# Two-layer decoder trunk on one core: five of sixteen expert pairs returned to the tokens by way of DRAM, and the later adaLN vectors computed on VectorE, ScalarE and GpSimd

## The chip, the core and the metric

One core of a Trainium2 chip runs the whole program. The metric is the device time of one execution in microseconds (us); the time before is the median of three. The engines are TensorE (PE, matrix products; its weight loads are listed as PEld), VectorE (DVE), ScalarE (ACT), GpSimd (POOL) and SyncE (SP), and sixteen DMA engines move data between DRAM and the on-chip memory. Each engine works through its own instructions in order and waits at semaphores for the others.

## What is computed

Two layers work on 512 tokens of width 1024 in float32. A conditioning vector gives six vectors (shift, scale and gate for the mixer, and for the experts) in each layer. A mixer of stick-breaking attention and gated linear attention follows, then 32 experts, of which each token uses two.

```python
def reference(x, c, w_ada, b_ada, norm_mix, norm_ffn, w_in, ...):
    c_act = jax.nn.silu(c)
    for l in range(DEPTH):
        mod = (c_act @ w_ada[l] + b_ada[l])[:, None, :]
        shift_m, scale_m, gate_m, shift_f, scale_f, gate_f = jnp.split(mod, N_MOD, axis=-1)
        h = rms_norm(x, norm_mix[l]) * (1.0 + scale_m) + shift_m
        x = x + gate_m * hybrid_mixer(h, w_in[l], ...)
        h = rms_norm(x, norm_ffn[l]) * (1.0 + scale_f) + shift_f
        x = x + gate_f * hierarchical_moe(h, ...)
    return x

# hierarchical_moe: comb is nonzero for two of the 32 experts of a token
    for g in range(N_GROUPS):
        a = jnp.einsum('nd,edf->nef', hf, w_gate[g])
        u = jnp.einsum('nd,edf->nef', hf, w_up[g])
        y = y + jnp.einsum('nef,efd->nd', jax.nn.silu(a) * u * comb[:, g, :, None], w_down[g])
```

## The kernel before

Each layer has a mixer stage and an expert stage.

**The mixer.** `project` cuts the input projection into steps of 128 rows of `w_in`. Two rows of steps share one load into a tile of the ring `raw` (4 tiles of 512 KB); ScalarE and VectorE split each part into a high and a low half, `whl` (lines 95 and 96), and TensorE multiplies (line 74). `mixer` walks through the steps: it loads 6 steps ahead, splits 2 steps ahead, runs the step, and advances the attention's generators. From step 12 on it also advances the generator `later`, which holds the conditioning vectors that are not needed at once: 12 chunks of 512 columns in layer 0 (eight of its own, four of layer 1) and 8 in layer 1. `paid` sets the pace, 1.1 pulls a step in layer 0 and 0.95 in layer 1.

A chunk is one call of `ada` (lines 220 to 256). It loads 2 MB of `w_ada` as four tiles `wada` of two row sets each. The first four chunks of layer 0 and six of layer 1 take them from the ring `mixs` (6 tiles), the others from `raw`, the ring of the projection's weights. TensorE then multiplies them by the conditioning vector in eight products, two passes each, that fill 32 rows of a PSUM bank each; ScalarE copies the bank to `row` (line 245), and a product with `sel` (ones in four rows) sums it and turns it into columns or into a broadcast row. A chunk takes five pulls.

**The experts.** Tokens are sorted into 64 slots for each expert; experts are handled in 16 pairs, so that a pair fills 128 rows. `fetch` gathers a pair's tokens by an indirect DMA of GpSimd from the DRAM copy `xg`. For a pair, `hidden` (`gu`, line 78) multiplies with both input matrices, `turn` transposes (`hsT`), and `down` (`d`) multiplies with the output matrix, weighted by the router into `o` (line 1057). `combine` brings a pair's result back to the tokens by TensorE: `o` is split into `ohi` (ScalarE, line 1062) and `olo` (GpSimd, line 1063), eight units of two products with the 0/1 matrix `oT` (`y`) follow, and VectorE adds each unit to `x` (line 1070). Within a layer the order is gu(0), d(0), gu(1), y(0), d(1), gu(2), y(1), and so on.

Weights stream on SP's queue in one fixed order, two input matrices `wgu` and then two output matrices `wd` for each pair, into 5 tiles of 2 MB and 4 tiles of 1 MB. A load is issued when the tile it takes has been read for the last time: `wgu` after the `gu` of its pair, `wd` after its `d`. A load that waits holds up all that stand behind it.

A scheduler sets the order of most instructions; those given to `pm` and `kept_dma`, the expert products among them, keep the order of the program.

Of the kernel before, what the change touches and what calls it, by code (L numbers as in the profile page):

```python
# [9 lines left out]
F = mybir.dt.float32  # L10
# [15 lines left out]
NX = 16  # L26


@with_exitstack
def hybrid_decoder_kernel(ctx, tc, x, c, w_ada, b_ada, norm_mix, norm_ffn, w_in, w_gk2, b_gk, q_gain,  # L30
# [182 lines left out]
    xg = dram.tile([S, D], F, name="xg")  # L213

# [8 lines left out]
    def ada(l, c0, n, raw, bank, at, later=True):  # L223

        vec, half = c0 // D, c0 % D // 512
        src = w_ada[l].rearrange("(p k) n -> p k n", k=KT)
        product = pm if later else mm
        ws, m = {}, 1024 // n
        for k in range(0, KT, m):
            w = raw([P, m, n], name="wada")  # L230
            (SY.dma_start if later else lambda *a: kept_dma(SY, *a))(w, src[:, k:k + m, c0:c0 + n])
            for i in range(m):
                ws[k + i] = w[:, i]
            if later and k % 4 == 2:
                yield
        if later and vec in (2, 5) and not half:
            gates[l, vec] = (gts if vec == 5 else gms[l])([P, D])
            kept_dma(G, gates[l, vec], along(b_ada, l * 6 * D + vec * D, D))
        yield
        row = rowt[at]([P, n], name="row")  # L240

        ps = bank("ada")
        for k in range(KT):
            product(ps[32 * (k % 4):32 * (k % 4) + 32, 0:n], ct1[:, k:k + 1].to_broadcast([P, 32]), ws[k], k < 4, k >= 4)
        A.copy(row, ps[:, 0:n])
        yield
        if vec in (2, 5):
            ps = bank("adaG")
            product(ps, sel, row, True, True)
            g = gates[l, vec][:, 512 * half:512 * half + 512]  # L250
            V.tensor_tensor(g, ps, g, op=OP.add)
        else:
            ps = bank("adaT")
            for i in range(n // P):
                product(ps[:, i:i + 1], row[:, P * i:P * i + P], sel[:, 0:1], i == 0, True)
            modulation(l, vec, slice(c0 % D // P, (c0 % D + n) // P), ps)
        yield
# [25 lines left out]
    def mixer(l, xt, ss, x_src, pool, later):  # L283
# [504 lines left out]
        for i, (weight, _, _, run) in enumerate(steps):  # L788
# [13 lines left out]
            if i >= 12:  # L802
                paid += 0.95 if l else 1.1
                while paid >= 1:
                    paid -= 1
                    next(later, None)
# [53 lines left out]
    def moe(l, xt, ss, pool):  # L860
# [176 lines left out]
        def down(hT, ws, i=None):  # L1037
# [7 lines left out]
            for q in range(2):  # L1045
# [5 lines left out]
                o = ot([P, 512], name="o")  # L1051
# [43 lines left out]
        def combine_last(pairs):  # L1095
# [18 lines left out]
            for n, u in ((0, 5), (0, 6), (1, 0), (1, 1), (0, 7), (1, 2), (1, 3), (1, 4), (1, 5), (1, 6), (1, 7)):  # L1114
                unit(n, u)

# [82 lines left out]
        with tc.issue_after(listed.ins), tc.issue_after(normed.ins):  # L1199
# [16 lines left out]
            dump(f"cw{l}", cw)  # L1216
            exw = tmp.rearrange("p t k e -> p (t k) e")
# [22 lines left out]
        hs = None  # L1240
        for i in range(NE // 2):
# [8 lines left out]
            if i:  # L1250
                part = places(i - 1), down(hT, [loaded.pop((1, e)) for e in (2 * i - 2, 2 * i - 1)], i - 1)
            *_, hs = hidden(gT1 if i == 1 else now, 0 if i < 2 else P * (i % 2), [loaded.pop((0, e)) for e in (2 * i, 2 * i + 1)])
# [3 lines left out]
            if i == NE // 2 - 1:  # L1256
                break

            if i == 0:
                for _ in second:  # L1260
                    pass
                weights_by_slot()
            for u in range(4):
                for v in range(2):
                    if i:
                        combine(2 * u + v, *part)
                next(rest, None)
                if u == 2:
                    hT = turn(hs)
        last = []  # L1270
# [95 lines left out]
```

## Time and profile before

| what | us |
|---|---|
| median of three runs | 1231.82 (1229.91 to 1234.94) |
| the profiled execution | 1231.71, of which span 1229.6 |
| PE busy | 1176.4 (96%) |
| DVE busy | 687.8 (56%) |
| ACT busy | 472.6 (38%) |
| POOL busy | 188.2 (15%) |

The span is the time from the first to the last instruction of the profiled execution. Busy time counts the stretches in which an engine works on at least one instruction; matrix products overlap, so a group's mean duration is longer than the time between two of them. The profile cuts the span into 40 slices: TensorE is at nine tenths or more in nearly all, and the DMA engines are at that in the two expert stages (some 390 to 600 us and 980 to 1200 us) and moderate in the mixers.

### The profile page before, as it was taken

The numbers are of one execution on the slowest core, as the hardware profiler recorded it, in microseconds if no ns is written. First come the engines' busy times: TensorE is split into PE (matmuls) and PEld (weight loads), VectorE is DVE, ScalarE is ACT, GpSimd is POOL, SyncE is SP. The second block draws the span as 40 slices with busy tenths as digits, with TensorE's granted clock in tenths as the row PEclk, the third lists the DMA queues.
The fourth block names the chain that finished last, engine by engine and source line by source line (L and its number), as shares of the span: only waits on it lengthen the run. The fifth ranks groups of instructions, "written<-read, shape, count | busy, mean of one in ns | idle before, by whom it ended". The sixth has DMA issues, their size and how long they took to land. (4 is left out here: it accounts for less than half of the span.)

```text
span 1229.6 us, 17212 instructions
## 1 busy us (share of the span) xinstructions
PE 1176.4 (96%) x6441; PEld 743.4 (60%) x6441; DVE 687.8 (56%) x1343; ACT 472.6 (38%) x940; POOL 188.2 (15%) x222
## 2 busy tenths in 40 slices
PE   4999999999989999999999997999999999999996
PEld 2687766666765444444478785666776744444443
DVE  4475545465864555555566563445846565555553
ACT  4376646453242111111155764454624411111111
POOL 1000010011302222221110001001310222222110
PEclk8999999999999999999999999999999999999999
DMA  9653665643687999999445354564129599999981
GB/s 299 211 181 110 202 166 155 198 152 96 258 353 265 410 411 420 420 419 418 178 168 167 96 172 108 171 179 127 56 103 383 212 397 420 420 418 420 420 328 69
DMA packets 105902, 312.27 MB, mean 254 GB/s; under 512 B 12852, under 2 KB 49912, under 8 KB 81240
## 3 DMA queue, kind: packets, MB, share of 16 engines
q1 hardware_dynamic: 96920, 289.62, 63.3%
q0 software_dynamic: 8896, 21.52, 5.2%
q8 instruction: 52, 0.85, 0.3%
q14 instruction: 34, 0.28, 0.1%
HBM read 311.08 MB, written 8.40 MB: 260 GB/s over the span
## 5 line engine op out<-in xcount | busy, mean ns | idle before, releaser
L78 PE MATMUL gu<-wgu,gT 128*64 128x512 f32 x1024 | 225.4, 592 | 0.1
L74 PE MATMUL proj<-whl,hh 128*128 128x512 f32 (+2 forms) x768 | 220.6, 370 | 0.1
L78 PEld LDWEIGHTS gu<-wgu,gT 128*64 128x64 f32 x1024 | 75.4, 137 | 143.7 <-issue 142.2
L74 PEld LDWEIGHTS proj<-whl,hh 128*128 128x128 f32 x768 | 133.9, 190 | 35.0 <-issue 13.3
L1070 DVE TENSOR_TENSOR x<-y,x 128x512 f32<-128x512 f32 x240 | 148.2, 679 | 0.9 <-PE y L78 0.9
L74 PE MATMUL proj<-whl,hl 128*128 128x512 f32 (+2 forms) x384 | 138.6, 362 | 0.0
L1025 DVE TENSOR_TENSOR hs<-hs,gu 128x256 f32<-128x256 f32 x32 | 13.5, 421 | 201.2 <-ACT hs L1024 201.2
L78 PE MATMUL d<-wd,hT 128*64 128x512 f32 x512 | 116.9, 598 | 1.4 <-ACT hT L1034 1.4
L1063 POOL TENSOR_TENSOR olo<-o,ohi 128x512 fp32r<-128x512 f32 x60 | 77.0, 1285 | 263.4 <-ACT ohi L1062 263.4
L96 DVE TENSOR_TENSOR whl<-raw,whl 128x512 fp32r<-128x512 f32 (+2 forms) x128 | 73.2, 574 | 78.0 <-ACT whl L95 67.6
L78 PE MATMUL y<-ohi,oT 128*128 128x512 f32 x240 | 104.5, 436 | 0.0
L95 ACT ACTIVATE whl<-raw 128x512 fp32r<-128x512 f32 (+2 forms) x128 | 66.4, 524 | 76.6 <-PE proj L74 64.7
L78 PE MATMUL y<-olo,oT 128*128 128x512 f32 x240 | 94.2, 393 | 0.0
L74 PEld LDWEIGHTS proj<-whl,hl 128*128 128x128 f32 x384 | 72.4, 189 | 14.2 <-issue 4.3
L1024 ACT ACTIVATE hs<-gu 128x256 f32<-128x256 f32 x32 | 12.3, 385 | 168.4 <-PE gu L78 168.4
L78 PEld LDWEIGHTS d<-wd,hT 128*64 128x64 f32 x512 | 33.9, 136 | 62.2 <-issue 48.1
L78 PEld LDWEIGHTS y<-ohi,oT 128*128 128x128 f32 x240 | 45.4, 189 | 31.7 <-issue 26.0
L1003 ACT ACTIVATE gT<-g,mod 128x256 f32<-128x256 f32 (+1 forms) x72 | 39.0, 544 | 62.6 <-DVE gT L1005 62.3
L1062 ACT ACTIVATE ohi<-o 128x512 fp32r<-128x512 f32 x60 | 37.8, 630 | 61.7 <-DVE o L1057 61.7
L1057 DVE SCALAR_TENSOR_TENSOR o<-d,cws,gate_f 128x512 f32<-128x512 f32 x64 | 47.6, 746 | 21.4 <-PE d L78 21.4
L733 POOL TENSOR_TENSOR raw<-raw,gate_m 128x1024 f32<-128x1024 f32 x16 | 40.4, 2533 | 122.9 <-DMA raw<-in_w_out_dram 63.1
L78 PE MATMUL ada<-wada,ct 128*32 128x512 f32 x320 | 50.2, 600 | 5.3 <-DMA wada<-in_w_ada_dram 3.8
(332 smaller groups left out, 1935.0 us busy)
## 6 DMA issues: line engine op xcount, KB each, us to landing
wgu<-in_w_gate_dram SPq DMA_DIRECT2D x64, 1024.0 KB, 9.6
wgu<-in_w_up_dram SPq DMA_DIRECT2D x64, 1024.0 KB, 11.8
wd<-in_w_down_dram SPq DMA_DIRECT2D x64, 1024.0 KB, 11.0
wada<-in_w_ada_dram SPq DMA_DIRECT2D x96, 512.0 KB, 5.1
raw<-in_w_in_dram SPq DMA_DIRECT2D x80, 256.0 KB, 4.5
raw<-in_w_out_dram SPq DMA_DIRECT2D x16, 512.0 KB, 5.0
raw<-in_w_in_dram SPq DMA_DIRECT2D x32, 128.0 KB, 4.0
xg<-xn POOLq DMA_DIRECT2D x8, 512.0 KB, 5.9
```

Of the source, the lines that this page charges most:

```text
L74: T.matmul(o, a, b, start=start, stop=stop, skip_group_check=True)
L78: tc.keep_in_program_order(T.matmul(o, a, b, start=start, stop=stop, skip_group_check=True))
L95: A.activation(hi, src, AF.Copy)
L96: eng.tensor_tensor(lo, src, hi.bitcast(F), op=OP.subtract)
L733: G.tensor_tensor(t, t, gates[l, 2][:, None, cols].to_broadcast([P, 2, 512]), op=OP.mult)
L1003: A.activation(o, src, AF.Identity, scale=m, bias=b)
L1024: A.activation(hs[r], gu[r, 0:256], AF.Silu)
L1025: V.tensor_tensor(hs[r], hs[r], gu[r, 256:512], op=OP.mult)
L1057: V.scalar_tensor_tensor(o, pd, cws[:, i:i + 1], gate, op0=OP.mult, op1=OP.mult)
L1062: A.activation(hi, o, AF.Copy)
L1063: (G if last is None else V).tensor_tensor(lo, o, hi.bitcast(F), op=OP.subtract)
L1070: V.tensor_tensor(xc, ps, xc, op=OP.add)
```

## The change

In `ada`, the chunks that `later` pulls no longer use TensorE for the eight products. ScalarE scales the row sets 5, 6 and 7 in place, VectorE scales and adds row sets 0 to 4 into `row` (five instructions), and, one pull later, GpSimd adds the three others. The sum over partitions is the product with `ones` in the place of `sel`. A chunk takes six pulls, and the pace is 1.25 and 1.05.

In the experts, the first five pairs (`NY`) have no `combine`. Their `o` is written to a DRAM tensor `ys` by GpSimd's queue (two DMAs of 256 KB for a pair), and eight times late in the stage `take_back` gathers for 128 tokens the row of the first or second expert by an indirect DMA. Tokens whose row is not in `ys` have an index past the end, which is skipped, and a factor `ysm` of 0. VectorE adds the row to `x`. For these pairs `down` of pair i−1 stands behind `hidden` of pair i, not ahead of it.

```diff
+NY = 5
...
-        ps = bank("ada")
-        for k in range(KT):
-            product(ps[32 * (k % 4):32 * (k % 4) + 32, 0:n], ct1[:, k:k + 1].to_broadcast([P, 32]), ws[k], k < 4, k >= 4)
-        A.copy(row, ps[:, 0:n])
+        if later:
+            summed = ones
+            for k in range(5, KT):
+                A.activation(ws[k], ws[k], AF.Copy, scale=ct1[:, k:k + 1])
+            V.tensor_scalar(row, ws[0], ct1[:, 0:1], None, op0=OP.mult)
+            for k in range(1, 5):
+                V.scalar_tensor_tensor(row, ws[k], ct1[:, k:k + 1], row, op0=OP.mult, op1=OP.add)
+            yield
+            for k in range(5, KT):
+                G.tensor_tensor(row, row, ws[k], op=OP.add)
...
-                paid += 0.95 if l else 1.1
+                paid += 1.05 if l else 1.25
...
+                    if i < NY:
+                        kept_dma(G, ys[P * i:P * i + P, 512 * q:512 * q + 512], o)
+                        continue
...
+        def take_back(tt, k):
+            r = rows_([P, D], name="back")
+            G.indirect_dma_start(r, None, ys[:, :], bass.IndirectOffsetOnAxis(ap=ysi[:, tt, k:k + 1], axis=0),
+                                 bounds_check=NY * P - 1, oob_is_err=False)
+            xc = xt[tt // 2][:, tt % 2]
+            return lambda: V.scalar_tensor_tensor(xc, r, ysm[:, tt, k:k + 1], xc, op0=OP.mult, op1=OP.add)
...
-            if i:
+            if i > NY:
                 part = places(i - 1), down(hT, [loaded.pop((1, e)) for e in (2 * i - 2, 2 * i - 1)], i - 1)
-            *_, hs = hidden(...)
+            *_, new = hidden(...)
             load_weights(4)
...
+            if i <= NY:
+                if i:
+                    hT = turn(hs)
+                for _ in range(4):
+                    next(rest, None)
+                if i:
+                    down(hT, [loaded.pop((1, e)) for e in (2 * i - 2, 2 * i - 1)], i - 1)
+                hs = new
...
+                continue
...
+                if i >= NE // 2 - 4 and u % 2 == 0:
+                    taken.append(take_back(*back.pop(0)))
+                    if len(taken) > 1:
+                        taken.pop(0)()
```

On TensorE, at the start of layer 1's expert stage (`gu`, `d` and `y` as above, `g` the transposes of fetched tokens, `hsT` those of the hidden rows, `lst` and `slots` the lists of slots), the order before is

```order
L78 MATMUL gu<-wgu,gT 64x512 x16
L997 MATMUL g<-ident,rows 128x128 x8
L78 MATMUL lst<-tmp,ohp 64x16 x16
L78 MATMUL slots<-dg,n_72 128x128 x8
L997 MATMUL g<-ident,rows 128x128 x6
L1032 MATMUL hsT<-ident,hs 128x128 x2
L997 MATMUL g<-ident,rows 128x128 x2
L78 MATMUL d<-wd,hT 64x512 x8
L78 MATMUL gu<-wgu,gT 64x512 x16
L78 MATMUL y<-ohi,oT 128x512
L78 MATMUL y<-olo,oT 128x512
```

and now

```order
L80 MATMUL gu<-wgu,gT 64x512 x16
L1013 MATMUL g<-ident,rows 128x128 x8
L80 MATMUL lst<-tmp,ohp 64x16 x16
L80 MATMUL slots<-dg,n_72 128x128 x8
L1013 MATMUL g<-ident,rows 128x128 x8
L80 MATMUL gu<-wgu,gT 64x512 x16
L1048 MATMUL hsT<-ident,hs 128x128 x2
L1013 MATMUL g<-ident,rows 128x128 x8
L80 MATMUL d<-wd,hT 64x512 x8
L80 MATMUL gu<-wgu,gT 64x512 x16
```

The first `d` has moved behind the second `gu`, and no `y` follows. SP's order of the weight loads is the same in both.

On VectorE, in layer 0's mixer around the second half of the gate of the experts (`whl` the split of projection weights, `t` and `sl` steps of the attention, `gr` a copy out of PSUM), before:

```order
L96 TENSOR_TENSOR whl<-raw,whl 128x256
L524 SCALAR_TENSOR_TENSOR t<-z,t 128x384
L96 TENSOR_TENSOR whl<-raw,whl 128x256
L96 TENSOR_TENSOR sl<-t,sh 128x384
L96 TENSOR_TENSOR whl<-raw,whl 128x256 x3
L251 TENSOR_TENSOR gate_f<-adaG,gate_f 128x512
```

and now

```order
L98 TENSOR_TENSOR whl<-raw,whl 128x256
L249 TENSOR_SCALAR row<-wada,ct_118 128x512
L251 SCALAR_TENSOR_TENSOR row<-wada,ct_118,row 128x512
L267 TENSOR_TENSOR gate_f<-adaG,gate_f 128x512
L540 SCALAR_TENSOR_TENSOR t<-z,t 128x384
L251 SCALAR_TENSOR_TENSOR row<-wada,ct_118,row 128x512
L98 TENSOR_TENSOR whl<-raw,whl 128x256
L98 TENSOR_TENSOR sl<-t,sh 128x384
L251 SCALAR_TENSOR_TENSOR row<-wada,ct_118,row 128x512
L98 TENSOR_TENSOR whl<-raw,whl 128x256
L251 SCALAR_TENSOR_TENSOR row<-wada,ct_118,row 128x512
```

The five instructions of a chunk now stand between the splits on which TensorE's next steps wait.

On GpSimd, in the last third of layer 0's mixer (`sh` and `sl` are cleared for the attention, `raw<-raw,gate_m` weights the output projection), before:

```order
L528 MEMSET sh 128x128
L529 MEMSET sl 128x128
L528 MEMSET sh 128x128
L320 DMA gain<-in_q_gain_dram 64x1 x2
L320 DMA gain<-in_k_gain_dram 64x1 x2
L325 DMA wg_5687<-in_w_gk_dram 16x256
L529 MEMSET sl 128x128
L733 TENSOR_TENSOR raw<-raw,gate_m 128x1024 x4
```

and now

```order
L336 DMA gain<-in_k_gain_dram 64x1 x2
L254 TENSOR_TENSOR row<-row,wada 128x512 x3
L341 DMA wg_5534<-in_w_gk_dram 16x256
L545 MEMSET sl 128x128
L254 TENSOR_TENSOR row<-row,wada 128x512 x2
L749 TENSOR_TENSOR raw<-raw,gate_m 128x1024
L254 TENSOR_TENSOR row<-row,wada 128x512
L749 TENSOR_TENSOR raw<-raw,gate_m 128x1024 x2
```

The chunk's three additions stand in threes among the clears and the weightings.

## Rows read from the trace of the kernel before

**Rows 1.** Busy time by engine in four stretches, the conditioning chunks of layer 0 and of layer 1 and the expert stages of layer 0 and of layer 1: stretch in us, its length, then busy us and instructions of each engine, the granted clock of TensorE as a share of full speed, the DMA engines' share and GB/s.

```profile
90.00:310.00 220.00, 215.83 (x1248) 153.68 (x1246) 117.69 (x219) 118.65 (x234) 22.71 (x32) 1.00 0.51 155
683.00:846.00 163.00, 154.23 (x880) 110.33 (x879) 79.35 (x154) 89.84 (x180) 9.94 (x22) 0.98 0.51 147
388.00:606.00 218.00, 218.00 (x1042) 102.52 (x1040) 124.57 (x227) 42.38 (x84) 46.05 (x38) 1.00 0.97 400
976.00:1197.00 221.00, 220.76 (x1096) 106.20 (x1093) 124.93 (x231) 46.15 (x92) 46.94 (x39) 1.00 0.98 403
```

**Rows 2.** The chain of work that ended last, in order of time: start, us, what. One conditioning chunk, then layer 1's first pair, its second and third, and its last.

```profile
683.74 1.85 PE ada L78 x16
...
969.53 7.16 PE gu L78 x32
...
985.74 6.87 PE gu L78 x32
992.60 1.12 PE y L78 x4
993.95 0.94 PE y L78 x4
995.10 0.92 PE y L78 x4
996.47 0.92 PE y L78 x4
997.61 3.58 PE d L78 x16
1001.20 6.87 PE gu L78 x32
...
1201.29 6.87 PE gu L78 x32
```

**Rows 3.** Groups of instructions by line, over the whole span: line, engine, operation, out<-in, shapes, count, then busy us and mean ns of one, and idle us of the engine before them with what ended it.

```profile
L78 PE MATMUL ada<-wada,ct 128*32 128x512 f32 x320 | 50.2, 600 | 5.3 <-DMA wada<-in_w_ada_dram 3.8 <-ACT kt L647 1.5
L1063 POOL TENSOR_TENSOR olo<-o,ohi 128x512 fp32r<-128x512 f32 x60 | 77.0, 1285 | 263.4 <-ACT ohi L1062 263.4
L1062 ACT ACTIVATE ohi<-o 128x512 fp32r<-128x512 f32 x60 | 37.8, 630 | 61.7 <-DVE o L1057 61.7
L1082 DVE SCALAR_TENSOR_TENSOR oT<-slots_row,sid,o 128x512 fp32r<-128x512 f32 x32 | 23.7, 739 | 0.1
L245 ACT COPY row<-ada 128x512 f32<-128x512 f32 (+1 forms) x28 | 14.7, 526 | 58.4 <-PE ada L78 31.6 <-PE ada L74 24.7 <-DMA wada<-in_w_ada_dram 2.0
L687 DVE SCALAR_TENSOR_TENSOR gr<-gr,glag 128x1024 f32<-128x1024 f32 x4 | 4.9, 1215 | 0.0
```

**Rows 4.** What TensorE waited for in the chunks of layer 0 (first row) and of layer 1 (second row): us in total, times, longest.

```profile
PE ada L78 <- DMA wada<-in_w_ada_dram: 3.0, 5, 1.4
...
PE ada L78 <- DMA wada<-in_w_ada_dram: 0.8, 2, 0.6
```

**Rows 5.** Timeline of layer 0's mixer at 267 us: start, us, engine, line, operation, out<-in, shapes, and the idle time before it with its releaser.

```profile
267.57 2.38 POOL L733 TENSOR_TENSOR raw<-raw,gate_m 128x1024 f32<-128x1024 f32 x1 [6.55 <-DMA raw<-in_w_out_dram]
...
268.13 0.69 DVE L524 SCALAR_TENSOR_TENSOR t<-z,t 128x512 f32<-128x512 f32 x1 [2.77 <-ACT t L523]
...
268.74 1.77 DVE L685 TENSOR_TENSOR gr<-sg,gr 128x512 f32<-128x512 f32 x1
...
271.63 0.67 DVE L685 TENSOR_TENSOR gr<-sg,gr 128x512 f32<-128x512 f32 x1
```

**Rows 6.** Timeline of SP's queue in layer 1's expert stage: start of the issue, us, queue, line, out<-in, count.

```profile
976.64 0.33 SPq L884 DMA_DIRECT2D wgu<-in_w_gate_dram  x1
...
985.76 1.59 SPq L880 DMA_DIRECT2D wd<-in_w_down_dram  x2
992.63 0.33 SPq L884 DMA_DIRECT2D wgu<-in_w_gate_dram  x1
...
1178.15 0.33 SPq L884 DMA_DIRECT2D wgu<-in_w_gate_dram  x1
...
1186.74 0.80 SPq L880 DMA_DIRECT2D wd<-in_w_down_dram  x2
```

**Rows 7.** Busy time in three stretches of 20 us of layer 1's expert stage, columns as in the first group.

```profile
1020.00:1040.00 20.00, 20.00 (x97) 9.11 (x94) 9.10 (x17) 3.44 (x7) 4.54 (x4) 1.00 1.02 417
...
1160.00:1180.00 20.00, 20.00 (x97) 9.56 (x94) 9.96 (x18) 3.44 (x7) 2.55 (x2) 1.00 1.01 418
1180.00:1200.00 20.00, 20.00 (x96) 9.77 (x96) 13.77 (x25) 3.42 (x7) 2.86 (x2) 1.00 0.64 256
```

**Rows 8.** GpSimd's DMA queue over the span (packets, MB, share of 16 engines), then two kinds of DMA: KB of each and median us from issue to landing.

```profile
q0 software_dynamic: 8896, 21.52, 5.2%
...
wgu<-in_w_up_dram SPq DMA_DIRECT2D x64, 1024.0 KB, 11.8
...
rows<-xg,idx POOLq DMA_INDIRECT x32, 8.4
```

**Rows 9.** One late load of projection weights in layer 1's mixer: its place on the chain (start, us, what), what TensorE waited for in the chunks of that layer, and the engines' busy time around it, columns as in the first group.

```profile
752.59 12.30 DMA raw<-in_w_in_dram
```

```profile
PE qT L497 <- ACT w L550: 6.3, 1, 6.3
```

```profile
760.00:780.00 20.00, 13.67 (x64) 9.24 (x65) 7.23 (x13) 7.24 (x14) 3.62 (x6) 0.83 0.65 179
```

More of the change, by code (lines that the diff above doesn't have):

```diff
@@ L213, in hybrid_decoder_kernel @@
     xg = dram.tile([S, D], F, name="xg")
+    ys = dram.tile([NY * P, D], F, name="ys")
     mod = [const.tile([P, 6, KT], F, name=f"mod{l}") for l in range(L)]
@@ L240, in ada @@
         row = rowt[at]([P, n], name="row")
-        ps = bank("ada")
-        for k in range(KT):
-            product(ps[32 * (k % 4):32 * (k % 4) + 32, 0:n], ct1[:, k:k + 1].to_broadcast([P, 32]), ws[k], k < 4, k >= 4)
-        A.copy(row, ps[:, 0:n])
+        if later:
[8 more added lines that the diff above has]
+                G.tensor_tensor(row, row, ws[k], op=OP.add)
+        else:
+            summed = sel
+            ps = bank("ada")
+            for k in range(KT):
+                product(ps[32 * (k % 4):32 * (k % 4) + 32, 0:n], ct1[:, k:k + 1].to_broadcast([P, 32]), ws[k], k < 4, k >= 4)
+            A.copy(row, ps[:, 0:n])
         yield
@@ L248, in ada @@
             ps = bank("adaG")
-            product(ps, sel, row, True, True)
+            product(ps, summed, row, True, True)
             g = gates[l, vec][:, 512 * half:512 * half + 512]
@@ L254, in ada @@
             for i in range(n // P):
-                product(ps[:, i:i + 1], row[:, P * i:P * i + P], sel[:, 0:1], i == 0, True)
+                product(ps[:, i:i + 1], row[:, P * i:P * i + P], summed[:, 0:1], i == 0, True)
             modulation(l, vec, slice(c0 % D // P, (c0 % D + n) // P), ps)
@@ L1050, in down @@
                            ws[e][:, D * j + 512 * q:D * j + 512 * q + 512], j == 0, j == 1)
-                o = ot([P, 512], name="o")
+                o = (ohl if i is not None and i < NY else ot)([P, 512], name="o")
                 gate = gates[l, 5][r, 512 * q:512 * q + 512]
@@ L1115, in combine_last @@
                 unit(n, u)
+        ysi, ysm = pool.tile([P, NT, 2], I32, name="ysi"), t3(2, "ysm")
+        def take_back(tt, k):
[4 more added lines that the diff above has]
+            return lambda: V.scalar_tensor_tensor(xc, r, ysm[:, tt, k:k + 1], xc, op0=OP.mult, op1=OP.add)
         def spread(slot, slot0):
@@ L1216, in moe @@
             dump(f"cw{l}", cw)
+            V.tensor_scalar(ysi, slot, 65535.0, None, op0=OP.min)
+            V.tensor_scalar(ysm, slot, float(NY * P), None, op0=OP.is_lt)
             exw = tmp.rearrange("p t k e -> p (t k) e")
@@ L1239, in moe @@
         gT1, second = gather(fetched[1:2])
-        hs = None
+        hs, back, taken = None, [(tt, k) for tt in range(NT) for k in range(2)], []
         for i in range(NE // 2):
@@ L1248, in moe @@
                     fetched += [fetch(idx[:, j:j + 1]) for j in range(i + 4, min(i + 6, NE // 2))]
-            if i:
+            if i > NY:
                 part = places(i - 1), down(hT, [loaded.pop((1, e)) for e in (2 * i - 2, 2 * i - 1)], i - 1)
-            *_, hs = hidden(gT1 if i == 1 else now, 0 if i < 2 else P * (i % 2), [loaded.pop((0, e)) for e in (2 * i, 2 * i + 1)])
+            *_, new = hidden(gT1 if i == 1 else now, 0 if i < 2 else P * (i % 2), [loaded.pop((0, e)) for e in (2 * i, 2 * i + 1)])
             load_weights(4)
@@ L1262, in moe @@
                 weights_by_slot()
+            if i <= NY:
[5 more added lines that the diff above has]
+                    down(hT, [loaded.pop((1, e)) for e in (2 * i - 2, 2 * i - 1)], i - 1)
+                hs = new
+                if i == NY:
+                    hT = turn(hs)
+                continue
+            hs = new
             for u in range(4):
                 for v in range(2):
-                    if i:
-                        combine(2 * u + v, *part)
+                    combine(2 * u + v, *part)
+                if i >= NE // 2 - 4 and u % 2 == 0:
+                    taken.append(take_back(*back.pop(0)))
+                    if len(taken) > 1:
+                        taken.pop(0)()
                 next(rest, None)
@@ L1269, in moe @@
                     hT = turn(hs)
+        for (tt, k) in back:
+            taken.append(take_back(tt, k))
+        for add_back in taken:
+            add_back()
         last = []
```

## The prediction

> **What bounds the kernel now.** I read the engines' busy time by stretch first. In the stretch of layer 0's conditioning chunks TensorE is busy 215.83 of 220 us, in that of layer 1 154.23 of 163, while VectorE stands at 117.69 and 79.35 and the DMA engines at half [rows 1]. So the mixers end by TensorE, and work taken from it there is worth its own length, as long as whoever takes it over isn't late with what TensorE needs next. In the expert stages two things are full together: TensorE, 218.00 of 218 and 220.76 of 221 us, and the DMA engines, share .97 and .98 at 400 and 403 GB/s [rows 1]. Twenty-us stretches show a plateau of 417 and 418 GB/s, share 1.02 and 1.01, ending after 1180 us with 256 GB/s [rows 7]. The chain of waits names only TensorE there [rows 2], but that says who ended last, not that the loads would come sooner. This is the reading on which my forecast turns: less TensorE work in the expert stage doesn't shorten it by itself, because the weights come at the highest rate in the trace.
>
> **The conditioning chunks: taken away.** A chunk's sixteen products take 1.85 us on the chain [rows 2]; 320 products are twenty chunks [rows 3], so 37.0 us go: 12 chunks or 22.2 us in layer 0, 8 chunks or 14.8 us in layer 1. TensorE's waits for `wada`, 3.0 and 0.8 us [rows 4], go with them: 40.8 us in all. The closing product with `ones` is that with `sel` before: nothing.
>
> **The conditioning chunks: added.** VectorE gets five operations of 128x512 a chunk. The near rows are 0.739 us (`oT`), half of 1.215 us for twice the columns [rows 3], and 0.69 us with an input in PSUM [rows 5]; I take 0.74, so 3.7 us a chunk, 44 us in layer 0 and 30 in layer 1. ScalarE gets three of about 0.63 us and loses one copy of 0.53 [rows 3], 1.4 us a chunk; at 118.65 of 220 and 89.84 of 163 [rows 1] it has room: nothing. GpSimd gets three additions of 1.285 us [rows 3], 3.86 a chunk, 46 and 31 us, beside 22.71 and 9.94 of its own [rows 1]: room too, but its clears for the attention and its weightings stand between those additions and wait up to 3.9 us for them.
>
> VectorE's load in layer 0 becomes 117.7 + 44 = 162 us in a stretch that would shrink to about 198 (82%), and in layer 1 79.4 + 30 = 109 in 148 (74%). It isn't full on average, yet the five operations stand between the splits `whl`, and TensorE's next step waits for a split. And there is a second cost: while GpSimd added or multiplied, a VectorE operation with two inputs in on-chip memory took 1.77 us instead of 0.67, one with a PSUM input its usual 0.69 [rows 5]. If GpSimd's time shut out VectorE's whole, layer 0 would hold 162 + 46 = 208 us in 198, more than there is; at half, 185 (93%), and layer 1 125 of 148 (84%). The bounds of what is given back are nothing and everything. I take the middle for layer 0, half of its 22.2 us, 11; a quarter of layer 1's, 4, where VectorE has a quarter of its time free.
>
> The Trainium skill, "SBUF — State Buffer", section "Who interferes with whom", says that a VectorE instruction with two inputs in on-chip memory contends with a GpSimd instruction that reads there, and that the loser blocks for the whole instruction instead of sharing. The row above, 1.77 against 0.67 us, agrees. The page's rule speaks against this change: by it the half that I take for layer 0 is the whole, which is rival B.
>
> The later chunks draw `wada` from the projection's ring `raw`. Before, a tile was free after TensorE's 1.85 us [rows 2]; now the tiles of sets 4 to 7 wait one pull more (220 us / 12 chunks / 6 pulls, 3.1 us) and for GpSimd's 3.9: about 5 us longer. In most places the loads run ahead by more. Where they don't, a late load costs what it cost at 765 us, 6.3 us, with 13.67 us of TensorE in a window of 20 and the clock at 0.83 of full speed, that is on average between its two levels [rows 9]. As cost I take half of one such, 3 us; the ends are 0 and ten chunks of it.
>
> Sum of the mixers: −40.8 + 11 + 4 + 3 = −22.8 us.
>
> **The experts.** For five pairs a layer `y` goes from TensorE: 1.12 + 0.94 + 0.92 + 0.92 = 3.9 us a pair [rows 2], 19.5 a layer, 39 in all. Also gone are the splits `ohi` and `olo` (ScalarE and GpSimd, beside other work: nothing). What comes instead is DMA. GpSimd's queue moved 21.52 MB in 5.2% of the span [rows 8], 63.9 us, so 0.337 MB a us. The rows written to `ys` are 5 x 512 KB, 2.62 MB: 7.8 us a layer. The rows gathered are at most 8 x 512 KB, 4.19 MB or 12.4 us; about 10 of 32 experts have theirs in `ys`, and what is skipped isn't moved, so 3.9 us. That lies on the engines that are full in the first and middle part; the gathers fall to the last four pairs, where the rate falls off.
>
> Then the weights' queue. The first `d` is now behind the second `gu`. Before, the output matrices' tiles were asked for at 985.76 us, just as that `gu` began at 985.74 [rows 2, 6]; now they wait until it has run and `d` has read them, some 3.6 + 6.9 − 3.9 us later than that, about 6. Behind them on the one queue stands the next `wgu`, issued at 992.63 us [rows 6]. Where the loads in flight last until then, nothing is lost; where not, up to 6 us of the plateau. Against it: with 3.9 us less of TensorE a pair, tiles come free sooner, and TensorE's start on the last pairs has slack. The last `wgu` was issued at 1178.15 us [rows 6] and lands some 11.8 us later [rows 8], near 1190, but the last `gu` started at 1201.29 [rows 2]: 11 us in which TensorE, not the loads, was behind. So each layer gains up to those 11, and loses up to 7.8 + 6, with the gathers' 3.9 in part: between −11 + 7.8 = −3 (nothing lost in the queue, gathers in the open tail) and +7 (13.8 + 3.9 − 11). I take the middle, +2, since no row tells how much stays in flight at that point: +4 for two layers. TensorE's pauses in the early pairs may lower its clock; since it would then be waiting for loads, I price that at nothing.
>
> The eight gathers a layer land in about 8.4 us like those of `rows` [rows 8], one ahead of its use; VectorE's eight additions of 128x1024 at 1.215 us [rows 3], 10 us a layer, meet 125 us of 218 [rows 1]: nothing, but for the last, which can stick out by a few us at the end of a stage; that lies within the range.
>
> **Forecast.** The profiled execution took 1231.71 us, the median 1231.82, so they are one for this purpose. 1231.7 − 22.8 + 4 = 1213 us.
>
> **The rivals.**
> - A, the cover holds: VectorE and the ring give nothing back. For it: VectorE at 74 and 82% on average, and splits two steps ahead. Against it: the late load at 765 us shows that this pipeline has thin places [rows 9]. 1231.7 − 40.8 + 4 = 1195 us.
> - B, GpSimd shuts out VectorE for its whole 3.9 us a chunk: layer 0 gives nothing (208 us in 198), layer 1 half (140 us in 148), about 8. For it: [rows 5]. Against it: in the same rows the operation with an input in PSUM kept its 0.69 us, and GpSimd would be busy in only 69 of 198 us of layer 0. 1231.7 − 8 + 4 = 1228 us. The skill's rule on contention, named above, would lead here.
> - C, slower: the ring. Tiles held 5 us longer make the projection's loads late, at 6.3 us each [rows 9]. Ten chunks use `raw`, eight in layer 0 and two in layer 1. If eight of them end so, 1195 + 8 x 6.3 = 1245 us (TensorE waits, so VectorE catches up, and its give-back isn't added). It is slower than before from six on (6 x 6.3 = 37.8 against 36.8). For it: a price seen once. Against it: seen once, though the ring was shared before as well.
> - D, the loads are no ceiling: then `y` gives its full 39 us. Against it: share 1.01 to 1.02 [rows 7]. 1213 − 4 − 39 = 1170 us.
>
> **Chances.** Forecast 0.44, A 0.20, B 0.15, C 0.17, D 0.04. Within 0.5%, about what a measurement of this kernel can tell from no change, is 1225.5 to 1238. Faster: forecast, A and D, 0.68; same: B, 0.15; slower: C, 0.17. The range: the lower end is A and a little under it, 1193; the upper end takes in B, and C's eight events, 1246. D and the worst of C are left out. The forecast alone, by the bounds of the experts (−6 to +14 against +4) and of the give-back (±8), would be 1200 to 1225.
>
> **What would show it.** In the mixers: no `ada` products of sixteen; VectorE's busy time in these stretches at some 160 and 110 us (above 190 and 130 speaks for B, with a mean of the splits and additions well above their kind); shorter stretches, by some 11 and 11 us; projection loads on the chain, many of them, speak for C. In the experts: TensorE waiting for `wgu` in the first half, where it waited for nothing; the plateau unchanged at about 418 GB/s and longer; `wd` issued after the second `gu`; first to last `gu` at 1201.29 − 969.53 = 231.8 us before [rows 2], now 230 to 239 if I am right and about 212 if D is. I am wrong if the stage shortens by the 19.5 us of `y`, if the mixers keep their length with VectorE well under its limit, or if TensorE waits for raw loads in most chunks.

## The result, and the profile after

The changed kernel takes 1242.76 us (median of 15 runs, 1237.93 to 1250.78) against 1231.82 before: ratio 1.0096, 95% interval 1.0079 to 1.0114. It is slower. The profiled execution has a span of 1238.3 us, 8.7 more than before. From the starts of the first `proj` and the first `gu` of each layer, the stages are these (the last one runs to the end of the span):

| stage, us | before | after | difference |
|---|---|---|---|
| up to the first `proj` | 24.6 | 24.2 | −0.4 |
| mixer, layer 0 | 350.5 | 354.1 | +3.6 |
| experts, layer 0 | 262.4 | 267.8 | +5.4 |
| mixer, layer 1 | 332.0 | 326.9 | −5.1 |
| experts, layer 1 | 260.1 | 265.2 | +5.1 |

The mixers, of which I expected −22.8 us, gave 1.5 (and the start 0.4). The experts, of which I expected +4, cost 10.5. The stretches of the new kernel, columns as in [rows 1] (two in the mixers, two in the experts):

```profile
90.00:310.00 220.00, 199.24 (x1072) 157.25 (x1071) 169.23 (x270) 130.00 (x258) 67.20 (x64) 0.94 0.53 154
690.00:850.00 160.00, 144.29 (x800) 115.75 (x799) 109.91 (x193) 101.50 (x206) 32.23 (x38) 0.95 0.48 137
392.00:612.00 220.00, 207.81 (x960) 91.65 (x958) 97.64 (x164) 35.98 (x74) 48.30 (x46) 0.97 0.99 407
985.00:1200.00 215.00, 203.84 (x940) 92.79 (x940) 93.23 (x158) 36.66 (x75) 47.74 (x46) 0.98 0.99 407
```

TensorE now stands still for 20.8 of 220 us in layer 0's mixer, where it was 4.2 before. VectorE has 169.23 us instead of 117.69 there and 109.91 in layer 1; I had forecast some 160 and 110, and had named more than 190 and 130 as the sign of rival B. TensorE's mean granted clock over the span fell from 0.988 to 0.961: with pauses, it is at 0.94 and 0.95 of full speed where it was at 1.00 and 0.98 [rows 1]. In the experts TensorE waits and the DMA engines are at .99.

The groups of instructions that are new or have changed (columns as in [rows 3]):

```profile
L80 PE MATMUL gu<-wgu,gT 128*64 128x512 f32 x1024 | 243.7, 608 | 22.5 <-DMA wgu<-in_w_up_dram 21.1
...
L254 POOL TENSOR_TENSOR row<-row,wada 128x512 f32<-128x512 f32 x60 | 84.5, 1408 | 200.4 <-DVE row L251 70.8
...
L98 DVE TENSOR_TENSOR whl<-raw,whl 128x512 fp32r<-128x512 f32 (+2 forms) x128 | 86.7, 679 | 22.6 <-ACT whl L97 22.3
...
L251 DVE SCALAR_TENSOR_TENSOR row<-wada,ct,row 128x512 f32<-128x512 f32 x80 | 59.7, 747 | 26.0 <-DMA wada<-in_w_ada_dram 25.3
...
L248 ACT ACTIVATE wada<-wada,ct 128x512 f32<-128x512 f32 x60 | 42.5, 721 | 32.9 <-DMA wada<-in_w_ada_dram 31.2
```

The durations are near those I took (0.747 us for 0.74, 1.408 for 1.285). Two other things stand out. VectorE and ScalarE stood idle for 25.3 and 31.2 us in front of a chunk's instructions, waiting for `wada`; VectorE stood another 7.8 us in front of the first of its five (line 249). Before, TensorE waited 3.8 us for the products of these chunks, and ScalarE 2.0 in front of a copy [rows 3]. And the splits `whl`, unchanged by the edit, rose from a mean of 574 ns in the trace of before to 679. Both can be seen at work. The timeline of layer 0's mixer at 171 us (start, us, engine, line, operation; in brackets the idle time before it and its releaser):

```profile
172.31 4.11 DVE L98 TENSOR_TENSOR whl<-raw,whl 128x512 fp32r<-128x512 f32 x2
...
172.90 2.97 POOL L254 TENSOR_TENSOR row<-row,wada 128x512 f32<-128x512 f32 x2
...
175.93 0.72 PE L80 MATMUL adaT<-ones,row 128*128 128x1 f32 x5 [2.20 <-POOL row L254]
```

Two splits take 4.11 us beside GpSimd's two additions; alone, a split of that shape takes 0.69 (at 776.34 us, for one). TensorE's 2.20 us in the last row are a wait for GpSimd's sum itself; such direct waits are 2.4 us in all of layer 0's mixer. And the chain through layer 1's mixer (start, us, what):

```profile
762.10 0.67 DVE row L251
762.79 12.78 DMA wada<-in_w_ada_dram
775.68 0.72 ACT wada L248
776.83 1.11 PE qT L513 x4
```

with the timeline of the same time:

```profile
770.86 0.75 DVE L251 SCALAR_TENSOR_TENSOR row<-wada,ct,row 128x512 f32<-128x512 f32 x1 [6.01 <-DMA wada<-in_w_ada_dram]
771.52 0.42 DVE L98 TENSOR_TENSOR whl<-raw,whl 128x256 fp32r<-128x256 f32 x1
...
775.67 0.75 DVE L251 SCALAR_TENSOR_TENSOR row<-wada,ct,row 128x512 f32<-128x512 f32 x1 [3.07 <-DMA wada<-in_w_ada_dram]
775.68 0.72 ACT L248 ACTIVATE wada<-wada,ct 128x512 f32<-128x512 f32 x1 [8.77 <-DMA wada<-in_w_ada_dram]
```

Both engines stand at a conditioning load, and behind it in their order stand a split and the attention's `w`, for which TensorE's `qT` waits. It is at the same time as the late load of [rows 9]; there TensorE lost 6.3 us to one late load, and now it stands idle for 8.7 (768.2 to 776.8).

In the experts, SP's queue (layer 1; columns as in [rows 6]) and the engines' busy time from 20 us after the first `gu`:

```profile
981.50 0.67 SPq L900 DMA_DIRECT2D wgu<-in_w_up_dram  x1
997.42 0.83 SPq L896 DMA_DIRECT2D wd<-in_w_down_dram  x2
998.30 0.49 SPq L900 DMA_DIRECT2D wgu<-in_w_gate_dram  x1
```

```profile
993.00:1013.00 20.00, 17.00 (x84) 6.40 (x82) 5.80 (x10) 3.15 (x7) 4.26 (x6) 1.00 0.81 299
1013.00:1033.00 20.00, 15.47 (x66) 6.01 (x68) 2.90 (x5) 1.77 (x4) 3.27 (x4) 0.89 1.01 421
```

The output matrices are asked for 24.4 us after the first `gu` (973.07), against 16.2 before [rows 2, 6], and the rate dips to 299 GB/s; the trace of before has 397 in the same 20 us (990 to 1010). From then on the rate is at its ceiling, and the chain runs through loads:

```profile
998.84 14.46 DMA wgu<-in_w_up_dram
...
1026.74 20.31 DMA wgu<-in_w_up_dram
...
1186.20 21.78 DMA wgu<-in_w_up_dram
1208.12 7.05 PE gu L80 x30
```

From the first `gu` to the last it now is 233.7 us, within the 230 to 239 that I had forecast; it was 231.6 by the same measure.

### The profile page after: what moved, and what is told of

It reads as the page before. It is cut to its first block, busy times and chain, and to the rows that moved or that the text cites. A ratio compares the mean times of both kernels' runs of the same rounds, so it can differ in the third digit from the quotient of the medians.

```text
span 1238.3 us, 16466 instructions
## 1 busy us (share of the span) xinstructions
PE 1127.7 (91%) x5961; PEld 733.7 (59%) x5961; DVE 747.8 (60%) x1363; ACT 480.5 (39%) x960; POOL 279.2 (23%) x298
## 5 line engine op out<-in xcount | busy, mean ns | idle before, releaser
L80 PE MATMUL gu<-wgu,gT 128*64 128x512 f32 x1024 | 243.7, 608 | 22.5 <-DMA wgu<-in_w_up_dram 21.1
L254 POOL TENSOR_TENSOR row<-row,wada 128x512 f32<-128x512 f32 x60 | 84.5, 1408 | 200.4 <-DVE row L251 70.8
L1089 DVE TENSOR_TENSOR x<-y,x 128x512 f32<-128x512 f32 x160 | 99.7, 680 | 1.6 <-PE y L80 1.6
L98 DVE TENSOR_TENSOR whl<-raw,whl 128x512 fp32r<-128x512 f32 (+2 forms) x128 | 86.7, 679 | 22.6 <-ACT whl L97 22.3
L1082 POOL TENSOR_TENSOR olo<-o,ohi 128x512 fp32r<-128x512 f32 x40 | 53.9, 1351 | 122.7 <-ACT ohi L1081 109.8
L251 DVE SCALAR_TENSOR_TENSOR row<-wada,ct,row 128x512 f32<-128x512 f32 x80 | 59.7, 747 | 26.0 <-DMA wada<-in_w_ada_dram 25.3
L80 PE MATMUL y<-ohi,oT 128*128 128x512 f32 x160 | 69.9, 437 | 0.4 <-DVE x L1089 0.4
L993 POOL DMA_INDIRECT rows<-xg,idx x32 | 33.6, 1051 | 143.0 <-PE g L1013 125.4
L80 PE MATMUL y<-olo,oT 128*128 128x512 f32 x160 | 63.1, 394 | 0.8 <-POOL olo L1082 0.8
L248 ACT ACTIVATE wada<-wada,ct 128x512 f32<-128x512 f32 x60 | 42.5, 721 | 32.9 <-DMA wada<-in_w_ada_dram 31.2
```

The source lines that it names most:

```text
L80: tc.keep_in_program_order(T.matmul(o, a, b, start=start, stop=stop, skip_group_check=True))
L98: eng.tensor_tensor(lo, src, hi.bitcast(F), op=OP.subtract)
L248: A.activation(ws[k], ws[k], AF.Copy, scale=ct1[:, k:k + 1])
L251: V.scalar_tensor_tensor(row, ws[k], ct1[:, k:k + 1], row, op0=OP.mult, op1=OP.add)
L254: G.tensor_tensor(row, row, ws[k], op=OP.add)
L993: G.indirect_dma_start(r, None, xg[:, :], bass.IndirectOffsetOnAxis(ap=idx, axis=0), bounds_check=S - 1, oob_is_err=False)
```

## Experiments

Times are medians, ratios are to runs of the kernel before on the same chip, with their 95% intervals. "Q" below is the theory that a chunk's instructions in VectorE's and ScalarE's order, with the loads they wait for, stop TensorE; "P" that GpSimd's reads lengthen VectorE's; "R" that tiles of the ring are held too long.

**The two parts by themselves.** `e1_ada_alone` is the kernel before with the new `ada` and its pace; `e2_experts_alone` the changed kernel with the old `ada` and its pace.

> The conditioning chunks as in the changed kernel, the experts as before. By stages of the two traces the chunks are worth -0.4 + 3.7 us in layer 0's mixer and -5.1 in layer 1's, and the experts +10.4, so if the parts are independent: 1230, within 2 us of before. If the experts' order disturbs the mixers (what is left on the queues when a mixer starts), it is clearly below: 1215 to 1222.

> The experts as in the changed kernel, the conditioning chunks on TensorE as before. If the parts are independent: 1231.8 + 10.4 = 1242, with TensorE waiting for wgu in the first half of the stage and the plateau at 418 to 422 GB/s. If the loss in the experts came from mixers that leave the weights later or earlier, it is nearer to before: 1234 to 1237.

Measured: e1 1230.70, ratio 0.9997 (0.9983 to 1.0012); e2 1238.23, ratio 1.0056 (1.0036 to 1.0076). So the new chunks gain nothing, and the experts cost some 7 us. The product of the two ratios is 1.0053; the whole change is at 1.0096. Some 4 or 5 us more belong to the two together.

**What TensorE's share is worth.** In `e3_sum_left_out`:

```diff
-            for k in range(5, KT):
-                A.activation(ws[k], ws[k], AF.Copy, scale=ct1[:, k:k + 1])
-            V.tensor_scalar(row, ws[0], ct1[:, 0:1], None, op0=OP.mult)
...
+            A.copy(row, ws[0])
             yield
-            for k in range(5, KT):
-                G.tensor_tensor(row, row, ws[k], op=OP.add)
```

> Like the chunks alone, but the weighted sum over the eight row sets is left out: a copy of the first set by ScalarE takes its place, the loads and the closing product stay. It shows what TensorE's sixteen products are worth when nobody takes them over. By the account of the prediction 1231.8 - 40.8 = 1191 to 1195. If the loads of the projection weights hold TensorE anyway, the gain is smaller, 1205 to 1220, and the loss of the change isn't due to who took the products over.

Measured: 1186.51, ratio 0.965 (0.963 to 0.967), 44 us. The prediction had 40.8. TensorE does bound the mixers, and taking over costs all of the 44. The busy times of e1 and then of e3:

```profile
PE 1144.8 (93%) x6121; PEld 748.9 (61%) x6121; DVE 780.6 (64%) x1443; ACT 493.4 (40%) x980; POOL 273.5 (22%) x282
```

```profile
PE 1128.2 (95%) x6121; PEld 738.9 (62%) x6121; DVE 679.1 (57%) x1343; ACT 467.9 (40%) x940; POOL 188.4 (16%) x222
```

The two profiled executions are 45.5 us apart (spans of 1229.1 and 1183.6). For the same 6121 products TensorE is busy 16.6 us longer in e1, and its mean granted clock is 0.974 against 0.982. So more than half of the loss is TensorE standing still, and the rest is products that take longer. VectorE has 101.5 us more in e1, of which its part of the sums is 72.6; its other work takes 28.9 us longer, about a third of the 85.2 us that GpSimd's additions last.

**Who costs them.** Five ways to take over, each on e1:

```diff
 e5_all_on_vector
-            for k in range(5, KT):
-                A.activation(ws[k], ws[k], AF.Copy, scale=ct1[:, k:k + 1])
...
-            for k in range(1, 5):
+            for k in range(1, KT):
                 V.scalar_tensor_tensor(row, ws[k], ct1[:, k:k + 1], row, op0=OP.mult, op1=OP.add)
             yield
-            for k in range(5, KT):
-                G.tensor_tensor(row, row, ws[k], op=OP.add)
 e6_none_on_vector: ScalarE scales all eight, GpSimd adds seven
 e9_reads_only: e5, and after the yield
+            for k in range(5, KT):
+                G.tensor_tensor(small([P, 512], BF, name="junk"), row, row, op=OP.add)
 e10_hold_only: e5, and after the yield
+            for k in range(5, KT):
+                G.tensor_tensor(tiny.tile([P, 1], F, name="held"), ws[k][:, 0:1], ws[k][:, 511:512], op=OP.add)
 e13_scalar_scales: ScalarE scales 5 to 7, V.tensor_tensor adds them ahead of the yield
```

> The chunks alone, but VectorE takes all eight row sets (eight operations a chunk), ScalarE and GpSimd none. VectorE gets three operations of some 0.70 us a chunk more, 42 us, and GpSimd's additions, beside which the splits rose from 0.574 to 0.697 us, are gone. If the contention with GpSimd's reads is what the chunks alone lost (44 us between 1230.7 and 1186.5): 1200 to 1215. If VectorE's own time, ahead of the splits, is it: 1240 to 1260. If the tiles held by GpSimd are it: 1210 to 1220.

> The chunks alone, but ScalarE scales all eight row sets (8 x 0.72 us a chunk) and GpSimd adds seven (7 x 1.41 us), VectorE none. If VectorE's own time in its order is the loss: 1195 to 1212. If it is the contention with GpSimd's reads (now seven a chunk and not three): 1240 to 1260. If it is the tiles held (now for 10 us by GpSimd): also 1240 to 1260, with raw loads late on the chain.

> All eight row sets on VectorE as in the run before (1210.9), and beside it three GpSimd additions a chunk that read the finished row twice and write a scratch tile nobody reads: GpSimd's reads come back, no load tile is held for them and nobody waits for their result. If the contention of GpSimd's reads with VectorE's is what the chunks lost between 1210.9 and 1230.7: 1225 to 1240. If the tiles held, or ScalarE's scaling, are it: 1209 to 1215.

> All eight row sets on VectorE, and one pull later three GpSimd operations of one column that read the tiles of sets 5 to 7 into a scratch tile nobody reads: the tiles are held into the next pull as in the change, GpSimd's long reads are absent. If the tiles' hold is the loss: 1222 to 1232. If it is contention or ScalarE's scaling: 1209 to 1214.

> ScalarE scales the sets 5 to 7 in place as in the change, but VectorE adds them at once, GpSimd none. It brings back ScalarE's three operations a chunk and their waits for wada (37 us in front of ScalarE's queue). If these are the loss, since the high halves of the splits stand behind them: 1222 to 1232. If GpSimd is (contention or hold): 1208 to 1215.

| run | us | ratio (95%) |
|---|---|---|
| e5, VectorE alone | 1210.89 | 0.9831 (0.9787 to 0.9874) |
| e6, none on VectorE | 1270.11 | 1.0304 (1.0258 to 1.035) |
| e9, e5 and GpSimd's reads | 1226.92 | 0.9978 (0.9957 to 0.9998) |
| e10, e5 and the hold | 1206.69 | 0.9815 (0.9786 to 0.9843) |
| e13, e5 with ScalarE's scaling | 1217.35 | 0.9871 (0.9842 to 0.99) |

VectorE's part of the sums takes 118.5 us in e5 and 72.6 in e1, 46 more, and yet the kernel is 20 us faster. e9 adds GpSimd operations that nobody waits for and that hold no load, and 16 us of the 20 are gone again. The busy times and the groups of e5 and then of e9:

```profile
PE 1138.7 (94%) x6121; PEld 744.9 (61%) x6121; DVE 787.3 (65%) x1503; ACT 458.5 (38%) x920; POOL 189.5 (16%) x222
...
L96 DVE TENSOR_TENSOR whl<-raw,whl 128x512 fp32r<-128x512 f32 (+2 forms) x128 | 73.1, 571 | 13.4 <-ACT whl L95 13.0
...
L247 DVE SCALAR_TENSOR_TENSOR row<-wada,ct,row 128x512 f32<-128x512 f32 x140 | 108.6, 777 | 24.3 <-DMA wada<-in_w_ada_dram 23.3
```

```profile
PE 1143.9 (94%) x6121; PEld 747.7 (61%) x6121; DVE 803.4 (66%) x1503; ACT 458.4 (37%) x920; POOL 265.7 (22%) x282
...
L96 DVE TENSOR_TENSOR whl<-raw,whl 128x512 fp32r<-128x512 f32 (+2 forms) x128 | 79.0, 618 | 10.3 <-ACT whl L95 10.1
...
L247 DVE SCALAR_TENSOR_TENSOR row<-wada,ct,row 128x512 f32<-128x512 f32 x140 | 112.1, 801 | 25.4 <-DMA wada<-in_w_ada_dram 24.6
...
L250 POOL TENSOR_TENSOR junk<-row 128x512 bf16<-128x512 f32 x60 | 73.8, 1230 | 161.4 <-DVE row L247 150.9
```

VectorE does the same 1503 instructions in both and is busy 16.1 us longer in e9, as much as the kernel loses. The splits go from a mean of 571 to 618 ns and the sums from 777 to 801. The mean hides that few are hit, and those hard, as the 4.11 us above. The rival is that GpSimd's own later work stands behind the added operations and that others wait for it. The traces leave it little room: in e9 TensorE's products wait for GpSimd nowhere, VectorE 1.8 us as in e5, and ScalarE 4.3 us, where it had no such wait in e5. So P is shown, but for some 4 us of the 16.

e10 excludes R, for a hold of one pull: it costs nothing. e13 falls between its two ranges. It lies 6 us above e5 by the medians, with intervals that overlap, and 11 above e10, with intervals that only just touch: ScalarE's scaling probably costs something. e6, above all of its ranges, doesn't separate contention from lateness, since TensorE's closing products wait there for GpSimd's sums themselves:

```profile
PE adaT L78 <- POOL row L250: 28.0, 8, 9.1
```

**The waits for loads.** `e7_pull_more` puts a `yield` ahead of e1's sum, at 1.46 and 1.23 pulls a step. `e14_no_late_loads` is e5 with `ws[k % 2]` for `ws[k]`. `e11_five_pulls` is e5 without the `yield` behind the sum, at 1.1 and 0.95.

> The chunks alone, with one pull more between the last load of a chunk and its sum, and the pace raised to match (seven pulls a chunk). If VectorE's and ScalarE's waits for wada at the head of their queues (21 us of VectorE's idle time) are a main part of the loss: 1212 to 1222. If VectorE's own time or the contention is: 1229 to 1233. If the tiles' hold is: 1235 to 1245.

> All eight operations on VectorE, but they read only the sets 0 and 1, the first load of a chunk; the sum over the other sets is left out, their loads stay. VectorE's time is that of the run with all eight on VectorE (1210.9), its waits for the later loads are gone. If VectorE's waits at the head of its queue are what is left of the loss: 1188 to 1198. If its own 5.9 us a chunk are: 1205 to 1211.

> All eight on VectorE, without the empty pull after the sum: five pulls a chunk at the pace of the kernel before. If the pace of the pulls matters little: 1207 to 1213. If the pull that is left out gave the sum time ahead of the closing product, on which TensorE then waits: 1214 to 1222.

Measured: e7 1235.36, ratio 1.0039 (1.0014 to 1.0064): a later sum doesn't help. The time lies in the range that I gave for the hold, which e10 excludes. Nor does it speak against Q: the added pull didn't shorten VectorE's waits for `wada`, which were 38.9 us against 30.9 in e1.

e14 took 1193.01, 0.9703 (0.967 to 0.9735), 18 us less than e5 and 6 more than e3. VectorE's waits for `wada` fell from 38.3 us to 17.5, all of them now for a chunk's first load. So of the 24 us between e5 and e3 some 18 go to the waits for the later loads, and some 6 are left for the first load and VectorE's own 5.9 us a chunk. One reservation: in e14 nobody reads the tiles of the sets 2 to 7, so they are also free sooner; that this is worth nothing is concluded from e10 and not shown by itself. The waits in e5, and then the sums' idle time in e14:

```profile
DVE row L247 <- DMA wada<-in_w_ada_dram: 23.3, 8, 8.9
DVE row L245 <- DMA wada<-in_w_ada_dram: 15.0, 5, 7.8
```

```profile
L247 DVE SCALAR_TENSOR_TENSOR row<-wada,ct,row 128x512 f32<-128x512 f32 x140 | 105.9, 757 | 0.8
```

e11 took 1204.52, 0.9773 (0.9747 to 0.9799), less than both of its ranges; the pull taken away costs nothing. With e17 below (0.9775) it is the fastest kernel here that leaves nothing out.

**Half of the chunks.** `e8_mixs_chunks_only` gives the new way to those chunks alone whose `ada` gets `mixs`.

> The chunks alone, but only those ten that load into the ring of their own (four of layer 0, six of layer 1) are summed by VectorE, ScalarE and GpSimd; the ten that load into the projection's ring stay on TensorE. If the loss comes from the shared ring (late loads, tiles held): the ten keep what TensorE loses, 10 x 1.85 us and some waits, 1208 to 1214. If each chunk loses what it gains wherever its tiles lie: 1229 to 1232.

Measured: 1244.11, ratio 1.01 (1.0054 to 1.0147), slower than with all twenty. None of the theories gives that. The chunks that load into `raw` run through their five pulls at the raised pace of 1.25 and 1.05 here, so two things differ from before, and this run settles nothing. The expectation, like the description of the kernel, has the two layers the wrong way round: by the kernel's `4 if l else 6` the first six chunks of layer 0 and the first four of layer 1 use `mixs`, and in this run's trace VectorE sums six chunks in layer 0 and four in layer 1. There are ten of either kind all the same.

**The experts.** `e4_no_traffic` is e2 without the writes to `ys` and `take_back`, `e15_no_gathers` without `take_back`, and `e16_d_first`:

```diff
+            if 0 < i <= NY:
+                down(hT, [loaded.pop((1, e)) for e in (2 * i - 2, 2 * i - 1)], i - 1)
             *_, new = hidden(...)
...
             if i <= NY:
-                if i:
-                    hT = turn(hs)
                 for _ in range(4):
                     next(rest, None)
-                if i:
-                    down(hT, [loaded.pop((1, e)) for e in (2 * i - 2, 2 * i - 1)], i - 1)
                 hs = new
-                if i == NY:
-                    hT = turn(hs)
+                hT = turn(hs)
                 continue
```

> Like the experts alone, but the first five pairs' results are dropped: no writes to ys, no gathers, no additions of rows; these tokens' parts are left out of the result. Theory that the loads bound the stage and the new traffic is what costs: 1231.8 - 1 to + 3, within 0.3% of before, some 8 us faster than the experts alone. Theory that the order (d behind the second gu, the queue of the weights) costs: still above 1237. Theory that TensorE's y would be worth its 39 us: near 1200.

> The experts alone with the writes to ys, but without the gathers and VectorE's additions of rows; the parts of these tokens are left out of the result. By the estimate of the prediction the writes cost 7.8 us a layer and the gathers 3.9: 1221.2 + 15.6 = 1237. If the gathers and the additions at the end are the larger part: 1224 to 1230.

> The experts alone, with down of pair i-1 ahead of hidden of pair i for the first five pairs too, as before. If the wait of the weights' queue behind the second gu costs the 6 us a layer that the prediction feared: 1226 to 1230. If loads in flight cover it: 1237 to 1240, as the experts alone (1238.2).

| run | us | ratio (95%) |
|---|---|---|
| e2, the experts' part | 1238.23 | 1.0056 (1.0036 to 1.0076) |
| e4, without writes and gathers | 1221.15 | 0.9917 (0.9896 to 0.9939) |
| e15, with writes, without gathers | 1238.95 | 1.007 (1.0045 to 1.0095) |
| e16, `d` first | 1227.10 | 0.9973 (0.9954 to 0.9992) |

The writes cost some 17 us, the gathers nothing that can be seen, and the order some 11. The order was tried only with the writes in place. The 20 us stretch of the dip is at 414 GB/s with `d` first (e16, shown first), and still at 328 without traffic (e4): it is the order that empties the queue.

```profile
986.00:1006.00 20.00, 19.02 (x96) 7.46 (x94) 4.16 (x8) 3.35 (x8) 3.24 (x4) 1.00 1.01 414
```

```profile
980.00:1000.00 20.00, 18.61 (x89) 6.91 (x90) 5.11 (x9) 2.80 (x6) 1.98 (x2) 1.00 0.86 328
```

Where the loads end shows the gathers: from 1192 to 1212 us e2 moves 344 GB/s and e15 263, as much as some 3.9 us at the ceiling move, without effect on the end.

**Together.** `e12_vector_and_experts` is the changed kernel with e5's sums, `e17_both_mended` e16 with e11's, and `e18_in_two_parts` e17 with a `yield` ahead of k = 4 in the sum, at 1.25 and 1.05.

> The whole changed kernel with all eight row sets on VectorE. If the parts are independent: 1210.9 + 7.4 (the experts alone) = 1218. The changed kernel is 5 us above the sum of its parts taken alone (1242.8 against 1230.7 + 7.4); if that comes from GpSimd's additions, this run has none of it; if from the chunks' early loads against the experts' traffic, 1223.

> The changed kernel with both parts mended: the chunks' sums on VectorE alone in five pulls, and down of pair i-1 ahead of hidden of pair i. If the parts are independent: 1204.5 - 3.8 = 1200.7. If the experts' part gains nothing once the mixers hand over earlier, or the chunks disturb its loads: 1204 to 1210.

> The run beside it, with VectorE's eight operations of a chunk in two halves: sets 0 to 3 in one pull, 4 to 7 in the next (six pulls, pace 1.25 and 1.05), so that the later loads have a pull more before VectorE's queue comes to them. If its waits for those loads are the rest of the loss: 1188 to 1196. If the loads are late by a fixed order on the ring, and come later with the later pulls: 1199 to 1206.

Measured: e12 1223.15, ratio 0.9918 (0.9889 to 0.9947); e17 1205.35, 0.9775 (0.9747 to 0.9802); e18 1209.65, 0.9822 (0.9806 to 0.9838). e12's time is the one that I gave for chunks whose early loads meet the experts' traffic; nothing else tests that. GpSimd's and ScalarE's part in the chunks costs the changed kernel 1.8% (1.0096 less 0.9918). The experts' path with `d` first, 0.9973 by itself, adds nothing to e11's 0.9773. e18 is above both of its ranges: giving the later loads another pull doesn't help, and VectorE's waits for `wada` hardly fall with it, from 38.6 us in e17 to 34.4.

## Why the prediction was wrong

The sign was wrong: 1213 us forecast, 1242.8 measured. The step that failed is the wait: the forecast let TensorE's waits for `wada` vanish with its products, and they came back, longer, on VectorE and ScalarE. None of the rivals has this. Of their mechanisms only B's, GpSimd shutting out VectorE, was seen, and not at B's size. C's 1245 is the number nearest to the measured one, by luck: its mechanism didn't happen.

- **That the mixers are TensorE's**: right. 40.8 us were forecast for the products and their waits, 44 measured (e3).
- **"TensorE's waits for `wada` go with them"**: the step that failed without my seeing it. Before, a late conditioning load stopped TensorE for 3.8 us in all; now it stops the queues in which the projection's splits and the attention stand. By e14, with the reservation made there, some 18 us of the kernel's time lie in VectorE's waits. I counted the five operations between the splits by their length alone. That length, which I feared, is within the 6 us that e14 leaves, and that for eight operations.
- **What VectorE gives back, 11 and 4**: too little. Against these 15 us stand some 26: those 6, and some 20 by which the chunks with GpSimd's additions and ScalarE's scaling are worse than on VectorE alone although VectorE does less. Reads by GpSimd cost 16 of them by themselves (e9). The Trainium skill, "SBUF — State Buffer", section "Who interferes with whom", has the loser of such a pair blocked for the whole instruction; the 4.11 us for two splits, where 1.4 were due, agree. But the rule is about two instructions that meet. In all, VectorE's other work became 28.9 us longer (e1 against e3), a third of GpSimd's time, less than the half that I took and far less than B's whole. The mistake was the price of these us: I took them to fill VectorE's free time, but in e9 VectorE's 16.1 us cost the kernel as much. My reading, not shown by itself, is that the blocked operations are splits and steps of the attention, and not sums for which nobody waits yet.
- **The ring, 3 us**: nothing (e10). Rival C, which rested on it, is out. In the mixers of the changed kernel ScalarE's splits wait for `raw` nowhere, where they did for 11.8 us before (the row below this list). C's count for the layers was the wrong way round as well: six chunks of layer 0 and four of layer 1 use `raw`.
- **ScalarE at nothing**: probably too little; 6 us by the medians against e5, 11 against e10 (e13).
- **TensorE's clock**: the forecast had it in the late load alone. Of the 45.5 us between the traces of e1 and e3, 16.6 are products that take longer, at a mean granted clock of 0.974 against 0.982.
- So the term −22.8 of the mixers should have been about 0: 44 less 18 for loads, some 6 for VectorE's own time and some 20 for GpSimd and ScalarE. These come from different kernels and are no exact account.
- **The experts, +4**: the terms were right and the sum a little low. If the differences above add, half of them gives for one layer: writes 8.5 us (forecast 7.8), order 5.6 (forecast up to 6), gathers none (forecast 3.9 in part), and so for TensorE's `y` with its slack 3.7 − 8.5 − 5.6 = −10.4 (forecast up to −11). The middle that I took between "nothing lost in the queue" and "all of it" was +2; all of it, without the gathers, is +2.8, and measured was +3.7. That the loads bound the stage held: at 39 us less of TensorE, none of these runs gained more than 10.
- What stays open: why the two parts cost some 4 or 5 us more together than alone. e12, which has none of GpSimd's additions, lies nearly as much above the product of e5 and e2 (0.9918 against 0.9886). That speaks against the additions as the reason, though there the difference is within the intervals. Open is also why e8 is so slow.

```profile
ACT whl L95 <- DMA raw<-in_w_in_dram: 11.8, 3, 8.0
```

## What to carry to other kernels

When work leaves the engine that bounds a stage, its waits for data move too, and they land at the head of another engine's queue: price what stands behind them there, not only the added busy time. A kernel that leaves the moved work out costs one run and tells at once what the most is that can be won. Element-wise work isn't free on GpSimd just because GpSimd is idle; here VectorE alone did three fifths more of the sums and was 20 us faster.

## What was not expected of the hardware

GpSimd operations that nobody waits for, 60 of 1.23 us, cost 16 us of the whole time, a fifth of their own length (e9). Writing 2.62 MB a layer to DRAM beside the stream of weights cost 8.5 us, 0.31 MB a us, while the weights moved at 0.42; why the writes are dearer than their bytes is not shown.
